# Where the operands of TensorE's products begin in SBUF: alike modulo 512 bytes, or 64 bytes apart

## The chip, the core and the metric

The kernel runs on one core of a Trainium2 chip. The metric is the device time of one execution in microseconds; a comparison takes the median of several runs. TensorE (PE) multiplies a stationary operand of up to 128 columns, which a weight load (PEld) brings into the array, with a moving operand of up to 512 columns that is streamed past it. The sums go to PSUM. VectorE (DVE), ScalarE (ACT) and GpSimd (POOL) do the elementwise work, and SyncE (SP) issues most transfers.

## The reference

A decoder trunk of two layers over 512 tokens of width 1024, in float32. Both layers have an adaptive RMSNorm, a mixer, a residual, a second adaptive RMSNorm, a SwiGLU feed-forward of hidden width 2816 and a residual:

```python
h = rmsnorm(x, norm_mix_g[layer]) * (1.0 + scale_m) + shift_m
mixed = attention_head_groups(h, ...) if layer % 2 == 0 else gated_deltanet(h, ...)
x = x + gate_m * mixed
h = rmsnorm(x, norm_ffn_g[layer]) * (1.0 + scale_f) + shift_f
gate, up = jnp.split(h @ ffn_w_in[layer], 2, axis=-1)
x = x + gate_f * ((silu(gate) * up) @ ffn_w_out[layer])
```

Layer 0 mixes with 8 block-sparse and 8 stick-breaking attention heads, layer 1 with a gated delta rule of 8 heads (projections q, k, v, z, a short convolution, a triangular inverse for each block, a scan over four chunks of 128 tokens).

## The kernel before

Everything is held transposed, features on partitions and 512 tokens along the free dimension. A float32 product is made of three products of rounded float32 values (type fp32r): every operand is split into a high and a low part, and the kernel adds high×high (line 330), high weight×low activation (line 331) and low weight×high activation (line 333). A weight chunk is 1024 features × 128 outputs, eight slices `wh[:, k]` and `wl[:, k]` of 512 bytes to a partition, so it takes 24 products of 512 columns each, or 48 of 256 columns where a product is done in two halves of the tokens (`HALVES`).

`weight_plan` lists all chunks in order. `fetch` loads each into a `raw` tile (SP's queue), ACT writes `wh` (line 247) and DVE or POOL writes `wl` (lines 249 to 252). Tiles `raw` (3 buffers), `wh` and `wl` (2 each) are in the pool `wpool`. Chunks that are needed in both halves are kept in the pool `keep` on the right side of SBUF. For layer 0's attention the chunks are fetched by POOL (`eng == "d"`), and every third pair takes two `raw` buffers in place of `wh` and `wl`.

The activations: `hs` (tiles `hh`, `hl`, right side of SBUF) is the normalised input of layer 0's mixer, of layer 0's feed-forward and of the delta-net; in layer 1's feed-forward its tiles hold the first 8 hidden chunks. `hs1` (`h1h`, `h1l`, left side) is the input of layer 1's feed-forward, and `ah`, `al` (left side) are the hidden chunks of both feed-forwards. The attention's outputs and values are `ah`, `al`, `bh`, `bl`, also on the left.

A tile's address is the sum of what stands before it in its pool stack. In the built program of the kernel before:

- on the left (the weights in `wpool`, `h1h`, `ah` and the like) tiles begin at 32 modulo 512 bytes;
- on the right `hs` begins at 480 modulo 512, and so do the kept weights.

Offsets inside the tiles (a weight slice, a half of the tokens, a block of 128 tokens) are multiples of 512 bytes. So in `hs` times weights the stationary operand begins 64 bytes further on than the moving one (modulo 512), in `h1h` or `ah` times weights both begin alike, and where a weight is the moving operand and `hs` the stationary one (`vproj`, `zproj`, lines 711 to 713 and 1109 to 1111) the stationary one begins 64 bytes earlier.

The 512-column products with `hs` against weights are 12 chunks of the attention's projections, 40 of layer 0's feed-forward input, 22 of the delta-net's projections, and 8 of the 22 hidden chunks in 7 of 8 output chunks of layer 1's feed-forward.

Of the kernel before, what the change touches and what calls it, by code (L numbers as in the profile page):

```python
# [8 lines left out]
F32 = mybir.dt.float32  # L9
# [4 lines left out]
OP = mybir.AluOpType  # L14
# [43 lines left out]


AHEAD = 2  # L60
LAG = 3
# [16 lines left out]
def weight_plan(I):  # L78

    p = []

    def add(key, src, kc=KC, n=128, eng="a", keep=False):
        p.append((key, src, kc, n, eng, keep))

    def out(name, src, nsplit, parts, keep, spare=()):
        order = list(range(KC - nsplit)) + (1 if keep or spare else 2) * list(range(KC - nsplit, KC))
        for n in order:  # L90
            for a, b in parts:
                add((name, n, a), src[n][:, a:b], b - a,
                    keep="h" if n in spare else keep and n >= KC - nsplit)

# [6 lines left out]
    def vproj(name, i, eng="a"):  # L101
        for j in (0, 4):
            add((name, i, j), I[name][i][:, j:j + 4], 4, 256, eng)

# [9 lines left out]
    for i in 2 * first:  # L114
        add(("gdn_in", i), I["gdn_in"][i], eng=EK0)
    for i in range(8 + NFIRST_GDN, 16):
# [9 lines left out]
    for i in range(2):  # L126
        for n in range(KC):
            add(("gdn_out", n, 0), I["gdn_out"][n])
    ffn(1)
# [3 lines left out]
def build(nc, tc, I, O):  # L133
# [3 lines left out]
    with ctx:  # L137
# [50 lines left out]
        G.memset(ones, 1.0)  # L188
        epsc = const.tile([128, 2], F32, name="epsc")
        G.memset(epsc[:, 0:1], EPS)  # L190
        G.memset(epsc[:, 1:2], math.pi / 2)
        eps = epsc[:, 0:1]
        ident = cst("ident")
# [30 lines left out]
        G.tensor_tensor(adabg, adab1[:, 8:16], gmix[:, 0:8], op=OP.mult)  # L224

# [44 lines left out]
        def w_pair(keep, kc, n, turn=False):  # L270

            if turn:
                turns[0] += 1
            tags = (("raw", 3),) * 2 if turn and turns[0] % 3 == 0 else (("wh", 2), ("wl", 2))
            return [kpool[0].tile([128, kc, n], F32R, name=t, tag=t, bufs=4) if keep else
                    wpool.tile([128, kc, n], F32R, name=t, tag=tag, bufs=bufs)
                    for t, (tag, bufs) in zip(("wh", "wl"), tags)]

        def fetch():
            _, dram, kc, n, eng, keep = plan[len(loaded)]  # L280
            if eng == "d":

                h, l = w_pair(keep, kc, n, True)
                dmas.append(nc.gpsimd.dma_start(h, dram).ins)
# [6 lines left out]
            if keep == "h":  # L291
# [9 lines left out]
                return  # L301
            h, l = w_pair(keep, kc, n)
            split(raw, h, l, eng)
# [225 lines left out]
def attention(e, x0ctx):  # L529
    nc, tc, V, G, A, PE, I = e.nc, e.tc, e.V, e.G, e.A, e.PE, e.I  # L530
    from contextlib import ExitStack
    with ExitStack() as ctx:
# [203 lines left out]
        def moba(pair, h, q, k):  # L736

            ph = work.tile([128, 1920], F32R, name="ph", tag="ph", bufs=1)
            pl = work.tile([128, 1920], F32R, name="pl", tag="pl", bufs=1)
            for i in range(4):  # L740
# [22 lines left out]
                e.split(src, *(x[:, i * 128:i * 128 + 384 * (i + 1)].rearrange("p (j q) -> p j q", q=384)[:, :, :128]  # L763
                               for x in (ph, pl)))
            pv_out(pair, h * 64, "m", ph, pl, lambda x, j: x[:, 512 * j:512 * j + 512 - 128 * j])
# [537 lines left out]
```

## Time and profile before

| | |
|---|---|
| median of 3 runs | 1423.26 us (1421.87 to 1425.09) |
| the profiled execution | 1422.44 us |
| its span in the trace | 1420.7 us |
| mean granted TensorE clock | 0.986 of full speed |
| PE busy | 1374.8 us, 97% of the span, 7354 products |
| DVE, ACT, POOL busy | 819.5, 605.7, 291.5 us |

A product's busy time in the trace overlaps that of the next one, so a product's pace is read from start to start: the distance between the starts of two products, divided by the number of products from the one to the other. Windows of the span are given in microseconds from its start.

### The profile page before, as it was taken

What the parts mean: (1) busy time and instruction counts of PE and PEld (TensorE: products, weight loads), DVE (VectorE), ACT (ScalarE), POOL (GpSimd) and SP (SyncE); (2) the same over time, 40 slices, a digit from 0 to 9 for tenths busy, and PEclk for the clock granted to TensorE, in tenths of its full rate; (3) what the DMA queues carried; (4) which work ended last, traced back from release to release, by engine and by line L of the source; (5) the groups of instructions that cost most, each with busy time, mean ns of one, the idle gap of its engine ahead of it and who ended that gap; (6) DMA issues with size and microseconds to landing.
All of it is one profiled execution on the core that took longest, in us unless ns stands there. A gap on an engine that the chain in (4) does not pass through costs nothing.

```text
span 1420.7 us, 19227 instructions
## 1 busy us (share of the span) xinstructions
PE 1374.8 (97%) x7354; PEld 1161.3 (82%) x7354; DVE 819.5 (58%) x1422; ACT 605.7 (43%) x1162; POOL 291.5 (21%) x280
## 2 busy tenths in 40 slices
PE   7899999899999999999999999999999999999997
PEld 4797777798888888889888778888998888888887
DVE  6777879654666666423777796446783333333233
ACT  5577888743222222223556643346662222222222
POOL 4024443110111111000024834311001111110010
PEclk8999999999999999999999999999999999999999
DMA  9437664141666676434522324312451323333332
GB/s 370 157 79 191 178 176 150 53 154 60 208 213 235 224 242 219 129 108 140 163 85 75 90 69 124 100 50 90 143 185 60 104 89 104 91 102 93 95 99 70
DMA packets 58734, 190.66 MB, mean 134 GB/s; under 512 B 7081, under 2 KB 11305, under 8 KB 58642
## 3 DMA queue, kind: packets, MB, share of 16 engines
q1 hardware_dynamic: 53376, 173.56, 37.7%
q0 software_dynamic: 4112, 14.82, 4.7%
q8 instruction: 58, 0.95, 0.3%
q10 hardware_dynamic: 1154, 1.05, 0.2%
q14 instruction: 34, 0.28, 0.1%
HBM read 184.11 MB, written 5.29 MB: 133 GB/s over the span
## 4 chain that ended last, share of the span: by engine, by line
PE 84%; DVE 5%; ACT 4%; DMA 3%; POOL 1%; issue 1%; SPq 0%; DVEq 0%; ACTq 0%; POOLq 0%
PE mm L330 21%; PE mm L331 21%; PE mm L333 21%; DMA wh<-in_attn_in_dram 2%; PE f L331 1%; PE f L330 1%; PE f L333 1%; PE mm L1111 1%; PE mm L1109 1%; PE mm L1110 1%; PE bank L943 1%; DVE DT L1003 1%; DMA call<-in_consts_dram 1%; PE bank L1045 1%; PE mm L712 1%
## 5 line engine op out<-in xcount | busy, mean ns | idle before, releaser
L247 ACT ACTIVATE wh<-raw 128x1024 fp32r<-128x1024 f32 (+1 forms) x203 | 211.4, 1041 | 544.1 <-PE mm L331 503.6
L252 DVE TENSOR_TENSOR wl<-raw,wh 128x1024 fp32r<-128x1024 f32 (+1 forms) x193 | 231.9, 1202 | 195.6 <-ACT wh L247 178.4
L330 PE MATMUL mm<-hh,wh 128*128 128x512 f32 (+1 forms) x776 | 292.6, 381 | 1.2 <-ACT wh L247 0.6
L331 PE MATMUL mm<-hl,wh 128*128 128x512 f32 (+1 forms) x776 | 291.0, 378 | 0.0
L333 PE MATMUL mm<-hh,wl 128*128 128x512 f32 (+1 forms) x776 | 245.7, 377 | 0.0
L330 PEld LDWEIGHTS mm<-hh,wh 128*128 128x128 f32 x776 | 146.7, 189 | 28.4 <-ACT wh L247 1.1
L331 PEld LDWEIGHTS mm<-hl,wh 128*128 128x128 f32 x776 | 146.5, 189 | 27.5
L333 PEld LDWEIGHTS mm<-hh,wl 128*128 128x128 f32 x776 | 141.9, 188 | 28.6
L249 POOL TENSOR_SCALAR ah<-ac 128x512 fp32r<-128x512 f32 x36 | 53.2, 1478 | 372.8 <-DVE ac L490 372.8
L212 DVE CUSTOM_DVE_ANT_0 aw<-aw,cond 128x1024 f32<-128x1024 f32 x96 | 126.2, 1332 | 5.8 <-DMA aw<-in_ada_w_dram 5.7
L331 PE MATMUL mm<-al,wh 128*128 128x512 f32 (+1 forms) x354 | 124.6, 356 | 0.0
L330 PE MATMUL mm<-h1h,wh 128*128 128x512 f32 x320 | 124.5, 389 | 0.0
L331 PE MATMUL mm<-h1l,wh 128*128 128x512 f32 x320 | 124.5, 389 | 0.0
L330 PE MATMUL mm<-ah,wh 128*128 128x512 f32 (+1 forms) x354 | 124.2, 356 | 0.2 <-ACT ah L247 0.2
L490 DVE TENSOR_TENSOR ac<-sg,mm 128x512 f32<-128x512 f32 x40 | 27.5, 688 | 152.4 <-PE mm L333 152.4
L333 PE MATMUL mm<-h1h,wl 128*128 128x512 f32 x320 | 105.0, 389 | 0.0
L333 PE MATMUL mm<-ah,wl 128*128 128x512 f32 (+1 forms) x354 | 104.1, 356 | 0.0
L330 PEld LDWEIGHTS mm<-ah,wh 128*128 128x128 f32 x354 | 66.7, 189 | 10.0 <-ACT ah L247 0.5
L331 PEld LDWEIGHTS mm<-al,wh 128*128 128x128 f32 x354 | 66.8, 189 | 9.5
L333 PEld LDWEIGHTS mm<-ah,wl 128*128 128x128 f32 x354 | 64.2, 189 | 9.5
L330 PEld LDWEIGHTS mm<-h1h,wh 128*128 128x128 f32 x320 | 60.1, 188 | 12.6
L333 PEld LDWEIGHTS mm<-h1h,wl 128*128 128x128 f32 x320 | 60.0, 188 | 12.5
(396 smaller groups left out, 2492.0 us busy)
## 6 DMA issues: line engine op xcount, KB each, us to landing
aw<-in_ada_w_dram SPq DMA_DIRECT2D x96, 512.0 KB
raw<-in_ffn_in_dram SPq DMA_DIRECT2D x88, 512.0 KB
raw<-in_ffn_out_dram SPq DMA_DIRECT2D x36, 512.0 KB
raw<-in_gdn_in_dram SPq DMA_DIRECT2D x26, 512.0 KB
raw<-in_gdn_z_dram SPq DMA_DIRECT2D x16, 512.0 KB
raw<-in_gdn_out_dram SPq DMA_DIRECT2D x16, 512.0 KB
raw<-in_ffn_out_dram SPq DMA_DIRECT2D x18, 384.0 KB
wh<-in_attn_in_dram POOLq DMA_DIRECT2D x12, 512.0 KB, 4.7
```

The costliest lines, as they stand in the source:

```text
L212: return V.tensor_tensor_reduce(w, w, cond, 1.0, 0.0, OP.mult, OP.add, mod[:, j:j + 1])
L247: ins = A.activation(h, src, AF.Copy)
L249: G.tensor_scalar(h, src, 1.0, 1.0, op0=OP.mult, op1=OP.mult)
L252: (G if eng == "p" else V).tensor_tensor(l, src, h.bitcast(F32), op=OP.subtract)
L330: PE.matmul(ps, wh[k][:, 0], xh[:, cs], start=first and i == 0, stop=False)
L331: PE.matmul(ps, wh[k][:, 0], xl[:, cs], start=False, stop=False)
L333: PE.matmul(ps, wl[j][:, 0], x[j][0][:, cs], start=False, stop=last and j == order[-1])
L490: ins = V.tensor_tensor(ac, sg, pu, op=OP.mult)
L712: PE.matmul(ps, xh[:, t], wl, start=False, stop=False)
L943: PE.matmul(ps[:, c], lhs[:, cs], rhs[:, cs], start=True, stop=True)
L1003: V.tensor_tensor(d, DS[:, :m, m:m + 1].to_broadcast([128, m, w]), DV[:, m:m + 1, m:].to_broadcast([128, m, w]), op=OP.mult)
L1045: PE.matmul(p4[:, c], U[h][lo, c], x[lo, c, lo], start=True, stop=True)
```

## The change

It adds 288 bytes of padding (`gap`) to the constants, takes a column of `epsc` and 88 columns of `adab1` away that nothing reads, and adds 448 bytes ahead of `keep`. With that every tile on the left moves from 32 to 480 modulo 512, and the kept weights from 480 to 32. The buffers `wh` and `wl` in `wpool` grow from 4096 to 4608 bytes, and a chunk begins `at` bytes into its buffer: 0 for the products of 512 columns, 64 for those of 256 columns, and 448 in `vproj`, where the weight is the moving operand. The output projections give `at=64` from chunk `KC - nsplit` on (the halves). To make room, `moba`'s tiles `ph` and `pl` shrink from 1920 to 1664 columns; their blocks stay where they were. No engine's order of instructions changes; POOL has one memset less.

After it, in the built program: `hs`, `h1h`, `ah` and all 512-column weights begin at 480 modulo 512; weights that are stationary in 256-column products begin at 32 (480 + 64); in `vproj` the moving weight begins at 416 and `hs` at 480. One case goes the other way: in the last output chunk of layer 1's feed-forward (`keep="h"`, 256 columns) the weights lie in `hs1`'s tiles. Before, they stood 64 bytes past `hs` for 8 of its hidden chunks (48 products), after it alike.

```diff
+GAP, GAP_KEPT = 288, 448
...
-    def add(key, src, kc=KC, n=128, eng="a", keep=False):
-        p.append((key, src, kc, n, eng, keep))
+    def add(key, src, kc=KC, n=128, eng="a", keep=False, at=0):
+        p.append((key, src, kc, n, eng, keep, at))
...
-                    keep="h" if n in spare else keep and n >= KC - nsplit)
+                    keep="h" if n in spare else keep and n >= KC - nsplit, at=64 if n >= KC - nsplit else 0)
...
-            add((name, i, j), I[name][i][:, j:j + 4], 4, 256, eng)
+            add((name, i, j), I[name][i][:, j:j + 4], 4, 256, eng, at=448)
...
     for i in 2 * first:
-        add(("gdn_in", i), I["gdn_in"][i], eng=EK0)
+        add(("gdn_in", i), I["gdn_in"][i], eng=EK0, at=64)
...
-            add(("gdn_out", n, 0), I["gdn_out"][n])
+            add(("gdn_out", n, 0), I["gdn_out"][n], at=64)
...
-        epsc = const.tile([128, 2], F32, name="epsc")
-        G.memset(epsc[:, 0:1], EPS)
-        G.memset(epsc[:, 1:2], math.pi / 2)
-        eps = epsc[:, 0:1]
+        eps = const.tile([128, 1], F32, name="eps")
+        G.memset(eps, EPS)
+
+        const.tile([128, GAP // 4], F32, name="gap")
...
-        adab1 = const.tile([128, 96], F32, name="adab1")
-        G.tensor_scalar(adab1, adab, 1.0, 1.0, op0=OP.mult, op1=OP.add)
+        adab1 = const.tile([128, 8], F32, name="adab1")
+        G.tensor_scalar(adab1, adab[:, 8:16], 1.0, 1.0, op0=OP.mult, op1=OP.add)
...
+            gap = kctx[0].enter_context(tc.tile_pool(name="gap", bufs=1, side="right"))
+            gap.tile([128, GAP_KEPT // 4], F32, name="gap")
             kpool[0] = kctx[0].enter_context(tc.tile_pool(name="keep", bufs=1, side="right", reuse_waits="tile"))
...
+            if keep:
+                return [kpool[0].tile([128, kc, n], F32R, name=t, tag=t, bufs=4) for t in ("wh", "wl")]
+            if turn and turns[0] % 3 == 0:
+                return [wpool.tile([128, kc, n], F32R, name=t, tag="raw", bufs=3) for t in ("wh", "wl")]
+            room = [wpool.tile([128, KC * 128 + 128], F32R, name=t, tag=t, bufs=2) for t in ("wh", "wl")]
+            return [t[:, at // 4:at // 4 + kc * n].rearrange("p (a b) -> p a b", b=n) for t in room]
```

## Rows read from the trace of the kernel before

**Rows 1.** The page: the span, TensorE's share, the chain that ended last.
```profile
span 1420.7 us, 19227 instructions
PE 1374.8 (97%) x7354; PEld 1161.3 (82%) x7354; DVE 819.5 (58%) x1422; ACT 605.7 (43%) x1162; POOL 291.5 (21%) x280
...
PE 84%; DVE 5%; ACT 4%; DMA 3%; POOL 1%; issue 1%; SPq 0%; DVEq 0%; ACTq 0%; POOLq 0%
```

**Rows 2.** Stages by windows: window, length, busy us by engine (count), granted clock, DMA.
```profile
core 0: us, PE busy (x) PEld busy (x) DVE busy (x) ACT busy (x) POOL busy (x), PEclk, DMA share, GB/s
...
40.00:67.00 27.00, 27.00 (x118) 21.84 (x117) 21.11 (x31) 13.26 (x24) 0.83 (x1) 1.00 0.48 153
...
100.00:293.00 193.00, 180.36 (x970) 146.25 (x970) 144.59 (x286) 147.73 (x333) 71.92 (x80) 1.00 0.56 157
...
345.00:567.00 222.00, 222.00 (x955) 178.93 (x954) 140.97 (x193) 51.01 (x59) 29.67 (x20) 1.00 0.64 215
...
811.00:876.00 65.00, 59.02 (x278) 48.27 (x277) 57.73 (x103) 26.64 (x41) 27.91 (x16) 0.95 0.30 91
...
1072.00:1290.00 218.00, 218.00 (x963) 180.48 (x962) 74.06 (x81) 52.10 (x60) 29.71 (x21) 1.00 0.30 94
```

**Rows 3.** The chain, 512-column products: start us, us, what.
```profile
354.27 0.93 PE mm L333 x4
...
567.07 0.93 PE mm L333 x4
...
597.04 0.91 PE mm L333 x4
...
656.88 0.91 PE mm L333 x4
...
1076.00 0.91 PE mm L333 x4
...
1184.80 0.91 PE mm L333 x4
1293.73 0.93 PE mm L333 x4
...
1369.43 0.93 PE mm L333 x4
```

**Rows 4.** Timeline of PE, `zproj`: start us, us, engine, line, what.
```profile
871.51 0.40 PE L1109 MATMUL mm<-wh,hh 128*128 128x512 f32 x1
...
874.04 0.39 PE L1111 MATMUL mm<-wl,hh 128*128 128x512 f32 x1
```

**Rows 5.** Timeline of PE, products of 256 columns in four places.
```profile
313.53 0.28 PE L330 MATMUL mm<-ah-1_176,wh 128*128 128x256 f32 x1
...
315.89 0.28 PE L333 MATMUL mm<-ah,wl 128*128 128x256 f32 x1
...
318.74 0.28 PE L330 MATMUL f<-hh,wh 128*128 128x256 f32 x1
...
319.70 0.28 PE L333 MATMUL f<-hh,wl 128*128 128x256 f32 x1
...
673.88 0.28 PE L330 MATMUL mm<-ah,wh 128*128 128x256 f32 x1
...
675.92 0.28 PE L333 MATMUL mm<-ah,wl 128*128 128x256 f32 x1
...
1014.57 0.62 PE L333 MATMUL mm<-hh,wl 128*128 128x256 f32 x4
...
1017.29 0.62 PE L333 MATMUL mm<-hh,wl 128*128 128x256 f32 x4
```

**Rows 6.** Windows of line 330 alone: PE busy us (count).
```profile
712.00:779.00 67.00, 31.27 (x78) 1.00 0.25 79
779.00:811.00 32.00, 13.55 (x33) 1.00 0.29 82
811.00:876.00 65.00, 26.62 (x65) 0.95 0.30 91
```

**Rows 7.** The chain of 100 to 293 us, shares by line.
```profile
by line: DMA wh<-in_attn_in_dram 11.5%; PE mm L330 7.0%; PE mm L331 6.8%; PE mm L333 6.5%; issue 6.3%; PE z L792 3.1%; ACT wl L285 2.8%; DVE aw L212 2.6%; PE o L723 2.5%; PE o L725 2.5%; ACT p L748 2.4%; ACT ph L247 2.3%; PE o L724 2.3%; DV
```

**Rows 8.** Timeline of the triangular inverse and its ends: POOL, DVE, transfer, PE.
```profile
781.11 3.10 POOL L983 TENSOR_SCALAR vp<-uv 32x128 f32<-32x128 f32 x8 [0.64 <-DVE uv L980]
...
811.25 0.16 POOL L999 MEMSET vp<- 128x32 f32 x1
...
811.45 0.21 DVE L1003 TENSOR_TENSOR DT<-vp 128x31 f32<-128x31 f32 x1 [2.91 <-POOL vp L999]
...
860.04 0.19 DVE L1005 TENSOR_TENSOR vp<-vp,DT 128x31 f32<-128x31 f32 x1
...
871.68 0.69 DVE L1018 TENSOR_TENSOR uv<-vp,call 128x512 f32<-128x512 f32 x1 [0.69 <-DMA vp<-dr]
...
875.86 0.38 PE L1028 MATMUL bank<-xinv,um 128*128 128x128 f32 x1 [1.43 <-DVE xinv L1022]
```

**Rows 9.** Timeline of PE, the second half of layer 0's first feed-forward chunks.
```profile
330.72 1.01 PE L330 MATMUL f<-hh,wh 128*128 128x256 f32 x4 [1.84 <-ACT hh L397]
```

More of the change, by code (lines that the diff above doesn't have):

```diff
@@ L218, in modcol @@
             return fin[:, j:j + 1]
-        adab1 = const.tile([128, 96], F32, name="adab1")
-        G.tensor_scalar(adab1, adab, 1.0, 1.0, op0=OP.mult, op1=OP.add)
+        adab1 = const.tile([128, 8], F32, name="adab1")
+        G.tensor_scalar(adab1, adab[:, 8:16], 1.0, 1.0, op0=OP.mult, op1=OP.add)
         adabg = const.tile([128, 8], F32, name="adabg")
-        G.tensor_tensor(adabg, adab1[:, 8:16], gmix[:, 0:8], op=OP.mult)
+        G.tensor_tensor(adabg, adab1, gmix[:, 0:8], op=OP.mult)
         def ada_fin1(comp, k):
@@ L264, in open_keep, with w_pair @@
             kctx[0] = ExitStack()
+            gap = kctx[0].enter_context(tc.tile_pool(name="gap", bufs=1, side="right"))
+            gap.tile([128, GAP_KEPT // 4], F32, name="gap")
             kpool[0] = kctx[0].enter_context(tc.tile_pool(name="keep", bufs=1, side="right", reuse_waits="tile"))
         turns = [0]
-        def w_pair(keep, kc, n, turn=False):
+        def w_pair(keep, kc, n, at, turn=False):
             if turn:
                 turns[0] += 1
[L274 to L277, printed above, removed]
+            if keep:
[4 more added lines that the diff above has]
+            return [t[:, at // 4:at // 4 + kc * n].rearrange("p (a b) -> p a b", b=n) for t in room]
         def fetch():
-            _, dram, kc, n, eng, keep = plan[len(loaded)]
+            _, dram, kc, n, eng, keep, at = plan[len(loaded)]
             if eng == "d":
-                h, l = w_pair(keep, kc, n, True)
+                h, l = w_pair(keep, kc, n, at, True)
                 dmas.append(nc.gpsimd.dma_start(h, dram).ins)
@@ L301, in fetch @@
                 return
-            h, l = w_pair(keep, kc, n)
+            h, l = w_pair(keep, kc, n, at)
             split(raw, h, l, eng)
@@ L736, in moba @@
         def moba(pair, h, q, k):
-            ph = work.tile([128, 1920], F32R, name="ph", tag="ph", bufs=1)
-            pl = work.tile([128, 1920], F32R, name="pl", tag="pl", bufs=1)
+            ph = work.tile([128, 1664], F32R, name="ph", tag="ph", bufs=1)
+            pl = work.tile([128, 1664], F32R, name="pl", tag="pl", bufs=1)
             for i in range(4):
@@ L762, in moba @@
                 src = pt[:, :n].rearrange("p (j q) -> p j q", q=128)
-                e.split(src, *(x[:, i * 128:i * 128 + 384 * (i + 1)].rearrange("p (j q) -> p j q", q=384)[:, :, :128]
-                               for x in (ph, pl)))
+                e.split(src, *(x.rearrange("p (j q) -> p j q", q=128)[:, i:4 * i + 1:3] for x in (ph, pl)))
             pv_out(pair, h * 64, "m", ph, pl, lambda x, j: x[:, 512 * j:512 * j + 512 - 128 * j])
```

## The prediction

> **What bounds the kernel now.** I read the page first: TensorE is busy 97% of the span, and 84% of the chain that ended last is on it [rows 1]. Shares are averages, so the windows came next [rows 2]. [...] From 100 to 293 us (attention) PE is busy 180.36 of 193.00 us and ACT and DVE about 145 each: a mixed chain. From 811 to 876 us DVE is busy 57.73 of 65.00 us and PE waits.
>
> So the question is what sets the pace. The chain gives it from start to start [rows 3]. In layer 0's feed-forward input (`hs` against weights, stationary operand 64 bytes further on) equal rows stand at 354.27 and 567.07 us with 38 chunks of 24 products between: 212.80 / 912 = 233.3 ns. In layer 1's (`h1h`, begins like the weights) they stand at 1076.00 and 1184.80 us, 20 chunks: 108.80 / 480 = 226.7 ns. The engines, shapes and clock are the same. The two output projections show it side by side: 66 products take 14.96 us in layer 0 (656.88 − 597.04, four chunks) where all operands begin alike, and 15.14 us in layer 1 (1369.43 − 1293.73, five chunks) where 24 of the 66 have `hs` as moving operand; the 0.18 us are 7.5 ns for each of the 24. At 256 columns it is the other way round [rows 5]: alike, 17 starts from 673.88 to 675.92 us are 120.0 ns apart; with the stationary operand 64 bytes on, 24 starts from 1014.57 to 1017.29 us are 113.3 ns apart. With the stationary operand 64 bytes earlier it is 230.0 ns at 512 columns (11 starts from 871.51 to 874.04 us [rows 4]) and 118.0 at 256 (20 starts from 313.53 to 315.89 us [rows 5]).
>
> I take it that the two start addresses modulo 512, one against the other, set the pace, and not the place of either: `hs` at 480 against kept weights at 480 paces 256 columns at 120.0 ns (8 starts from 318.74 to 319.70 us [rows 5]), the same as `ah` at 32 against weights at 32, and `hs` against weights at 32 paces them at 113.3.
>
> [...]
>
> **The change part by part.** A product gains 6.7 ns (233.3 to 226.7) at 512 columns with `hs`.
>
> - Layer 0's feed-forward input: 40 chunks × 24 = 960 products, PE saturated: 6.4 us.
> - Layer 1's feed-forward output: 7 chunks × 0.18 = 1.2 us.
> - Delta-net projections: 528 products. From 712 to 779 us line 330 alone runs 78 times [rows 6], so all three lines about 231 times, less 24 for the narrow a/b weights, whose offsets only turn round: 207 × 6.7 = 1.4 us, up to where POOL's copies start at 781.11 us [rows 8]. From there on a chain runs that holds no projection: POOL to 811.25, the 31 steps of DVE from 811.45 to 860.04, two transfers to 871.68, then DVE and the first product of the levels at 875.86 us, before which PE already waits 1.43 us. About (33 + 65) × 3 = 294 products lie beside it [rows 6]: 2.0 us that I count at nothing, for PE would just wait 3.4 us in place of 1.43. That is its upper bound. What is late next there is the DVE loop, as before.
> - Attention projections: 288 products, 1.9 us if all count, nothing if none. Lines 330, 331 and 333 hold 20.3% of the chain in 193 us, 39 us [rows 7], of which the attention's output chunks, alike already, take about 15; 24 us / 0.2333 is about 100 products, 0.7 us. I take 0.8.
> - Start: 118 products from 40 to 67 us with PE full [rows 2], about half with `hs` moving (6.7 ns), half with the weight moving (230.0 to 226.7, 3.3 ns): 0.6 us. Before 40 us PE waits for other work; nothing.
> - `zproj`: 192 products × 3.3 ns, less the 12 before the wait at 875.86: 0.6 us.
>
> At 256 columns the pace with 64 bytes is not one number: 113.3 ns is one chunk. I bound the gain from alike by 6.7 ns and, by the 118.0 of the other sign, by 2.0, and take 4.6, near the middle, because no row tells which chunk is typical (115.4 ns then).
>
> - Layer 0's feed-forward output, 264 products from 120.0 to 115.4: 1.2 us (0.5 to 1.8).
> - Attention output 192, layer 1's first feed-forward chunks 192, `vproj` 192, all from 118.0 to 115.4: 0.5 + 0.5 + 0.4 (0 to 2.7).
> - Layer 0's first feed-forward chunks, 192 products from 120.0: 0.9 us, but the first half lies before PE's wait of 1.84 us for the norm [rows 9], so 0.45.
> - The 48 products that lose their 64 bytes: −0.2 us.
>
> The rest costs nothing. POOL's memset less and the shorter add fall into the start, where transfers and the norm bind. The 4608-byte buffers hold the same bytes and the same writes; their only price is space. If ACT or DVE wrote slower at other addresses, which no row shows, it would be hidden: ACT is busy 51 of 222 and DVE 141 of 222 us in the longest stage [rows 2]; should that cover go, PE would wait there.
>
> Sum: 6.4 + 1.2 + 1.4 + 0.8 + 0.6 + 0.6 + 1.2 + 1.4 + 0.45 − 0.2 = 13.85 us. The profiled execution took 1422.44 us, so 1408.6; the median of the runs lies 0.82 higher, and I forecast **1409.4 us**, 1.0% faster. Differences within 0.2% (2.8 us) can't be told from none.
>
> **The rivals.**
>
> *All of it pays.* The 2.0 us beside the inverse, 1.1 more in attention, 0.4 in the start, 0.45 in the first chunks and the upper bounds at 256 columns (0.6 + 1.3) make 19.7 us: 1403.6 us. Against it stand the chains off PE in [rows 7, 8].
>
> *Only the saturated stages pay.* 6.4 + 1.2 + 1.4 + 0.5 − 0.2 = 9.3 us: 1414.0. For it: PE's slack in the other stages is filled by waits for ACT and DVE, which a faster PE only lengthens. Longer waits may also lower the clock: from 811 to 876 us, around a wait, the granted clock averages 0.95 against 1.00 [rows 2].
>
> *The moving operand's own place sets the pace* (the other side). At 480 (`hs`) 512 columns pace 233.3, at 32 (`h1h`, `ah`) 226.7. The change takes `h1h`, `ah` and the attention's outputs to 480: (320 + 242 + 20) × 3 = 1746 products would lose 6.7 ns, 11.7 us, `zproj` 0.6 more, all in saturated stages, and `hs` would gain nothing: 1423.3 + 12.3 = 1435.6 us. It decides from 1.6 ns a product on, where 1746 of them eat the 2.85 us that the 256-column terms give (1.2 + 1.4 + 0.45 − 0.2). Against it: the one tile `hs` at 480 has both paces at 256 columns, 120.0 and 113.3 [rows 5].
>
> *The addresses do not set the 512-column pace*, but something else that `hs` has, such as lying far up in SBUF. The 256-column terms alone might stay, 2.85 us, or nothing: 1420.4 to 1423.3, in the middle 1421.8. For it: no row has `hs` alike at 512 columns. [...] Against it, again the 256 columns, where `hs` alike behaves as `ah` alike.
>
> **How the numbers follow.** My forecast has 0.67; all of it pays 0.10; only the saturated stages 0.10; no effect at 512 columns 0.08; slower by the moving operand's place 0.05. The first three are faster: 0.87; the fourth is the same: 0.08; slower 0.05. The range takes in the forecast with its bounds and most of the next two cases, 1404 to 1415 us, and leaves the last two out.
>
> **What would show it.** In the changed kernel's chain, equal L333 rows in layer 0's feed-forward input should stand 5.44 us apart, as in layer 1's, in place of 5.60, and that stage should be 6.4 us shorter; layer 1's input should be as long as before. The output chunks of layer 1 should take 14.96 us. Chunks of `gdn_out` at 256 columns should stay as they are, and layer 0's output halves fall from 120.0 to between 113 and 118 ns. PE's wait before the first L1028 should grow by about 2 us, with the DVE loop as long as before. I am wrong if layer 1's feed-forward slows down, if layer 0's keeps 5.60 us, or if waits in attention eat more than the 1.9 us that it could gain.

## The result and the profile after

| | before | after |
|---|---|---|
| median | 1422.94 us (6 runs) | 1411.55 us (6 runs, 1410.65 to 1413.18) |
| ratio, 95% interval | | 0.992 [0.9907, 0.9933] |
| profiled execution | 1422.44 us | 1410.65 us |

The change saves 11.4 us by the medians and 11.8 between the two profiled executions, where the prediction summed 13.85 us. The time lies in the range that was given. Line numbers of the changed kernel stand 6 or 7 above those of before in the places spoken of here (L330, L331, L333 are now L337, L338, L340).

The page of the changed kernel, beside [rows 1]: the counts are those of before but for three instructions, the shares of the chain are within one per cent of those of before, and TensorE's busy time is 13.9 us less.

```profile
span 1408.8 us, 19224 instructions
PE 1360.9 (97%) x7354; PEld 1158.4 (82%) x7354; DVE 818.6 (58%) x1422; ACT 605.4 (43%) x1162; POOL 292.0 (21%) x279
...
PE 84%; DVE 6%; ACT 4%; DMA 3%; POOL 1%; issue 1%; SPq 0%; DVEq 0%; ACTq 0%; POOLq 0%
```

Its chain at four rows that answer to [rows 3] (start us, us, what): layer 0's feed-forward input 38 chunks apart, layer 1's feed-forward output 5 chunks apart.

```profile
352.82 0.91 PE mm L340 x4
...
559.54 0.91 PE mm L340 x4
...
1282.80 0.91 PE mm L340 x4
...
1357.60 0.91 PE mm L340 x4
```

The 38 chunks of layer 0 take 206.72 us where they took 212.80: 5.44 a chunk in place of 5.60, 226.7 ns a product in place of 233.3, and 40 × 0.16 = 6.4 us for the stage. The five output chunks of layer 1 take 74.80 us in place of 75.70; a chunk is 14.96, as in layer 0.

Four windows between the same products as in the kernel before (columns as in [rows 2]): the start, layer 0's first feed-forward chunks, its input, and the stage of the inverse.

```profile
40.70:68.42 27.72, 27.72 (x118) 22.77 (x117) 20.90 (x30) 12.62 (x23) 0.83 (x1) 0.95 0.45 145
...
316.72:343.78 27.06, 25.22 (x206) 24.65 (x204) 15.75 (x32) 12.82 (x23) 0.62 (x1) 1.00 0.25 79
343.78:559.60 215.82, 215.82 (x955) 178.73 (x954) 141.05 (x193) 51.09 (x60) 29.77 (x20) 1.00 0.66 221
...
800.25:867.09 66.84, 59.53 (x276) 49.56 (x275) 56.58 (x103) 26.65 (x41) 29.28 (x16) 0.92 0.31 91
```

Three of them show something beside the pace. The start did not get shorter (27.72 us; 27.00 for as many products in [rows 2]), but its granted clock averages 0.95 where it was 1.00. The first chunks of layer 0 took 1.94 us less, much more than their products could give. And from 800 to 867 us, where nothing was to be gained, 2 us were lost: 66.84 against some 65 in [rows 2]. Of these, 1.4 us lie ahead of DVE's first step of the inverse, because PE now reaches the window's first product earlier against it: 1.65 us ahead of that step (800.25 and 801.90 us), where it was 0.25 us ahead of it (811.20 and 811.45).

The window of the first chunks in the kernel before, at a granted clock of 0.94:

```profile
316.00:345.00 29.00, 27.16 (x205) 26.46 (x204) 15.77 (x32) 12.81 (x23) 0.62 (x1) 0.94 0.24 74
```

The timeline of PE at the products of 256 columns in layer 0's output halves (stationary operand 64 bytes on):

```profile
650.04 0.28 PE L337 MATMUL mm<-ah,wh 128*128 128x256 f32 x1
...
664.29 0.28 PE L338 MATMUL mm<-al,wh 128*128 128x256 f32 x1
664.41 0.59 PE L364 MATMUL mm<-ssq,ones 128*128 128x256 f32 x2
...
675.19 0.28 PE L340 MATMUL mm<-ah,wl 128*128 128x256 f32 x1
...
680.63 0.28 PE L340 MATMUL mm<-ah,wl 128*128 128x256 f32 x1
```

121 starts up to 664.29 us are 117.8 ns apart. Then two products of the norm come between, and 48 starts from 675.19 to 680.63 are 113.3 apart. Tiles, distance and clock are the same: one address distance has two paces here.

Last, the inverse in the changed kernel (timeline of PE, POOL and DVE), with the first full q/k/v product as a mark; it answers to [rows 8].

```profile
702.66 0.40 PE L338 MATMUL mm<-hl,wh 128*128 128x512 f32 x1
...
789.25 1.80 POOL L998 DMA_DIRECT2D dr<-vp  x1 [0.31 <-POOL vp L989]
...
796.60 0.60 POOL L999 DMA_DIRECT2D vp<-dr  x1 [1.84 <-DMA dr<-vp]
...
801.90 0.21 DVE L1009 TENSOR_TENSOR DT<-vp 128x31 f32<-128x31 f32 x1 [4.23 <-POOL vp L1005]
...
851.19 0.19 DVE L1011 TENSOR_TENSOR vp<-vp,DT 128x31 f32<-128x31 f32 x1
...
863.80 1.80 DVE L1024 TENSOR_TENSOR uv<-vp,call 128x512 f32<-128x512 f32 x1 [1.66 <-DMA vp<-dr]
...
866.88 0.38 PE L1034 MATMUL bank<-xinv,um 128*128 128x128 f32 x1 [1.82 <-DVE xinv L1028]
```

And three rows of the kernel before at the same places, which [rows 8] lacks:

```profile
712.08 0.40 PE L331 MATMUL mm<-hl,wh 128*128 128x512 f32 x1
...
799.73 1.80 POOL L992 DMA_DIRECT2D dr<-vp  x1 [0.31 <-POOL vp L983]
...
806.15 0.61 POOL L993 DMA_DIRECT2D vp<-dr  x1 [0.91 <-DMA dr<-vp]
```

From the mark to DVE's first step it is 99.24 us after and 99.37 before (811.45 − 712.08), so almost nothing came of a stage full of faster products. POOL waits 1.84 us for the first transfer in place of 0.91. From the end of DVE's last step (851.38 us; 860.23 before) to the returned blocks it is 12.42 us in place of 11.45. The transfers themselves have become slower (the first landed 7.1 us after its issue in place of 6.1, the last 7.4 in place of 6.4). The later return does not reach PE in this pair, though: its first product of the levels starts 15.50 us after DVE's last step (866.88 − 851.38), before it was 15.63 (875.86 − 860.23). The loop of DVE between took 49.48 us in place of 48.78; it takes 48.4 to 49.6 us in the executions of all kernels here.

### The profile page after: what moved, and what is told of

Its sections match the earlier page's. It is cut to its first block, busy times and chain, and to the rows that moved or that the text cites. A ratio compares the mean times of both kernels' runs of the same rounds, so it can differ in the third digit from the quotient of the medians.

```text
span 1408.8 us, 19224 instructions
## 1 busy us (share of the span) xinstructions
PE 1360.9 (97%) x7354; PEld 1158.4 (82%) x7354; DVE 818.6 (58%) x1422; ACT 605.4 (43%) x1162; POOL 292.0 (21%) x279
## 3 DMA queue, kind: packets, MB, share of 16 engines
q10 hardware_dynamic: 1154, 1.05, 0.2%
## 4 chain that ended last, share of the span: by engine, by line
PE 84%; DVE 6%; ACT 4%; DMA 3%; POOL 1%; issue 1%; SPq 0%; DVEq 0%; ACTq 0%; POOLq 0%
PE mm L337 21%; PE mm L338 21%; PE mm L340 21%; DMA wh<-in_attn_in_dram 1%; PE f L340 1%; PE f L338 1%; PE f L337 1%; PE mm L1117 1%; PE mm L1115 1%; PE mm L1116 1%; PE bank L949 1%; DVE DT L1009 1%; DMA call<-in_consts_dram 1%; PE bank L1051 1%; PE mm L719 1%
## 5 line engine op out<-in xcount | busy, mean ns | idle before, releaser
L254 DVE TENSOR_TENSOR wl<-raw,wh 128x1024 fp32r<-128x1024 f32 (+1 forms) x193 | 231.9, 1202 | 192.1 <-ACT wh L249 176.0
L337 PE MATMUL mm<-hh,wh 128*128 128x512 f32 (+1 forms) x776 | 290.0, 377 | 0.7 <-ACT wh L249 0.6
L338 PE MATMUL mm<-hl,wh 128*128 128x512 f32 (+1 forms) x776 | 288.0, 374 | 0.0
L340 PE MATMUL mm<-hh,wl 128*128 128x512 f32 (+1 forms) x776 | 243.2, 374 | 0.0
L337 PEld LDWEIGHTS mm<-hh,wh 128*128 128x128 f32 x776 | 146.6, 189 | 25.2 <-ACT wh L249 1.1
L338 PEld LDWEIGHTS mm<-hl,wh 128*128 128x128 f32 x776 | 146.9, 189 | 24.2
L340 PEld LDWEIGHTS mm<-hh,wl 128*128 128x128 f32 x776 | 142.7, 189 | 25.2
L338 PE MATMUL mm<-h1l,wh 128*128 128x512 f32 x320 | 124.5, 389 | 0.0
L337 PE MATMUL mm<-h1h,wh 128*128 128x512 f32 x320 | 124.5, 389 | 0.0
L338 PE MATMUL mm<-al,wh 128*128 128x512 f32 (+1 forms) x354 | 124.0, 355 | 0.0
L337 PE MATMUL mm<-ah,wh 128*128 128x512 f32 (+1 forms) x354 | 123.7, 355 | 0.2 <-ACT ah L249 0.2
L340 PE MATMUL mm<-h1h,wl 128*128 128x512 f32 x320 | 105.0, 389 | 0.0
L340 PE MATMUL mm<-ah,wl 128*128 128x512 f32 (+1 forms) x354 | 103.8, 355 | 0.0
L337 PEld LDWEIGHTS mm<-ah,wh 128*128 128x128 f32 x354 | 66.5, 188 | 9.9 <-ACT ah L249 0.5
L338 PEld LDWEIGHTS mm<-al,wh 128*128 128x128 f32 x354 | 66.6, 188 | 9.4
L340 PEld LDWEIGHTS mm<-ah,wl 128*128 128x128 f32 x354 | 63.9, 188 | 9.4
L338 PEld LDWEIGHTS mm<-h1l,wh 128*128 128x128 f32 x320 | 60.1, 188 | 12.5
L337 PEld LDWEIGHTS mm<-h1h,wh 128*128 128x128 f32 x320 | 60.0, 188 | 12.5
```

What stands on the lines that cost most here:

```text
L254: (G if eng == "p" else V).tensor_tensor(l, src, h.bitcast(F32), op=OP.subtract)
L337: PE.matmul(ps, wh[k][:, 0], xh[:, cs], start=first and i == 0, stop=False)
L338: PE.matmul(ps, wh[k][:, 0], xl[:, cs], start=False, stop=False)
L340: PE.matmul(ps, wl[j][:, 0], x[j][0][:, cs], start=False, stop=last and j == order[-1])
```

## Experiments

Each edit is one to the changed kernel, unless it says otherwise. Distances are those of the stationary operand's start past the moving one's.

**e1, the changed kernel again**, no edit.

> The changed kernel once more, for a second profile. The first profile gained 6.3 us in layer 0's feed-forward input and 1.2 us in layer 1's output, as forecast, but lost 1.4 us up to 67 us and 2.0 us between the start of DVE's inverse loop and the first product of the levels, where it was forecast to gain 0.6 and lose nothing. Theory L (where the half-clock stretches fall is chance): in a second profile the half-clock stretches lie elsewhere, the stages of pure products (layer 0's input 215.8 us, layer 1's output 93.8 us) repeat within 0.2 us, and the start or the inverse stage differs by 1 us or more from the first profile. Theory S (the faster products bring these losses with them): both stages repeat within 0.3 us and half-clock stretches lie at the same places.

One execution of 1410.89 us. The time of the stages of pure products came back to the hundredth of a microsecond (215.82 us in layer 0's input), as both theories had it. The stretch at half clock in the start came back at 41.0 us (40.3 in the first profile, granted 0.50 up to 43.7); products from 41.35 us on start 0.43 us apart, where those just before start 0.23 to 0.24 apart. The stage of the inverse took 0.4 us more than in the first profile. Of the 2.0 us that the expectation puts between DVE's first step and the first product of the levels, only 0.57 lay there in the first profile (64.98 us against 64.41); the rest lay ahead of that step.

**e2, the products of 512 columns alone**: the others get their old distances back, apart from the attention's output halves, which are alike here (and `open_keep` takes 0 in layer 0, 64 in layer 1).

```diff
-    keep="h" if n in spare else keep and n >= KC - nsplit, at=64 if n >= KC - nsplit else 0)
+    keep="h" if n in spare else keep and n >= KC - nsplit, at=0)
...
-            add((name, i, j), I[name][i][:, j:j + 4], 4, 256, eng, at=448)
+            add((name, i, j), I[name][i][:, j:j + 4], 4, 256, eng, at=64)
```

> The change for 512-column products alone: all of them alike modulo 512 as in the changed kernel; the 256-column products keep their distances of before (delta-net output and its first projections 64, vproj and layer 1's first feed-forward chunks the stationary operand 64 earlier, layer 0's output halves and first chunks alike), but for the attention's output halves, which are alike (before: 64 earlier; 192 products at 118.0 to 120.0 ns, 0.4 us worse). Theory A (both widths pay, each by its pace): 2.3 us of the 11.4 us belong to the 256-column products, so 1411.6 + 2.3 + 0.4 = 1414.3 us, ratio to before 0.994. Theory W (only the wide products pay, the 256-column stages gained by the clock): 1411.6 to 1412.0 us, ratio 0.992.

**e3, the products of 256 columns alone**: `hs` against 512-column weights is 64 bytes apart again, and the attention's output halves are alike (`open_keep` takes 384 in layer 1).

```diff
-GAP, GAP_KEPT = 288, 448
+GAP, GAP_KEPT = 352, 448
...
-            add((name, i, j), I[name][i][:, j:j + 4], 4, 256, eng, at=448)
+            add((name, i, j), I[name][i][:, j:j + 4], 4, 256, eng, at=384)
...
-            add(("gdn_out", n, 0), I["gdn_out"][n], at=64)
+            add(("gdn_out", n, 0), I["gdn_out"][n], at=0)
...
-        sm = gp.tile([128, 17, C4, HG], F32, name="sm")
+        sm = gp.tile([128, 16, C4, HG], F32, name="sm")
```

> The change for 256-column products alone: their distances as in the changed kernel (64), but for the attention's output halves, which are alike; 512-column products keep the distances of before (hs 64, weights moving in zproj 64 earlier, the others alike). A small tile that nothing reads is left out to make room. Theory A: 1422.9 - 2.3 + 0.4 = 1421.0 us, ratio 0.9987, and layer 0's feed-forward input at 5.60 us a chunk as before. Theory W: 1422.9 us, ratio 1.000. If the gains of e2 and e3 add up to that of the whole change (11.4 us, less the 0.4 us that each lacks twice), the two parts are independent.

e2 took 1415.12 us (0.9949 [0.9937, 0.9962]), e3 1417.83 (0.9971 [0.9961, 0.9981]): by the kernel before in the same series, 1422.88, they save 7.8 and 5.0 us, together 12.8 where the whole saves 11.4. Windows of layer 0's feed-forward input and of the second part of its output halves, in e2 and then in e3 (between the same products, 222.14 and 18.96 us before, 215.82 and 18.08 after):

```profile
345.52:561.35 215.83, 215.83 (x955) 178.80 (x954) 140.98 (x193) 51.10 (x60) 29.71 (x20) 1.00 0.66 221
665.22:684.18 18.96, 18.96 (x157) 18.85 (x156) 14.71 (x25) 13.08 (x21) 0.11 (x1) 1.00 0.62 182
```

```profile
343.49:565.61 222.12, 222.12 (x956) 179.01 (x954) 141.01 (x193) 51.11 (x60) 29.76 (x20) 1.00 0.64 215
669.28:687.50 18.22, 18.22 (x157) 18.11 (x156) 14.28 (x24) 13.16 (x20) 0.11 (x1) 1.00 0.60 181
```

In these windows each half moves its own stage and leaves the other's where it was before. The address distance is the cause, in both widths. e2's time is near its first theory's (1414.3 us). e3 saved more than either theory gave it (1421.0 or 1422.9), and two things in it and in e2 are not the products' pace. One is the granted clock in layer 0's first chunks: e2 has the old distance there (alike), and takes, between the same products as the 29.00 us of before,

```profile
318.02:345.52 27.50, 25.66 (x205) 25.08 (x204) 15.59 (x32) 12.81 (x23) 0.62 (x1) 1.00 0.27 78
```

So 1.50 us of the 1.94 are the clock, and 0.44 (27.50 − 27.06) the products. The gain by the clock is in e2, in e3 and in the whole change, so it counts twice in the 12.8. The other is the place of the delta-net's tiles (see e10 and e12): in e3 they begin at 384 modulo 512 and not at 448.

**e4, a sweep of distances**, in steps of 64 bytes over layer 0 and of 16 over layer 1.

```diff
-        for j in first + [j + f for f in range(NFIRST, FC) for j in (0, FC)]:
-            add(("ffn_in", l, j), I["ffn_in"][l, j], keep=j in first)
+        for c, j in enumerate(first + [j + f for f in range(NFIRST, FC) for j in (0, FC)]):
+            add(("ffn_in", l, j), I["ffn_in"][l, j], keep=j in first, at=16 * ((c - 4) % 32) if l else 64 * ((c - 4) % 8))
...
-            add(("gdn_out", n, 0), I["gdn_out"][n], at=64)
+            add(("gdn_out", n, 0), I["gdn_out"][n], at=64 * n)
```

> The changed kernel with other offsets of the weights, chunk by chunk: layer 0's feed-forward input (512 columns, hs moving) steps the distance of stationary from moving operand by 64 bytes from 0 to 448, five times round; layer 1's (512 columns, h1 moving) by 16 bytes from 0 to 496; the delta-net's output (256 columns, hs moving) by 64 bytes, twice round; zproj (512 columns, weight moving) by 64 bytes. Theory R (the distance modulo 512 sets the pace): the chunk time in layer 0 repeats every eight chunks; distance 0 gives 5.44 us for 24 products (226.7 ns), 64 gives 5.60 (233.3), 448 gives 5.52 (230.0), and the other five lie between 5.4 and 5.7, each the same in all five rounds within 0.03 us; layer 1 has the same time at the same distance. Theory P (the moving operand's or the weight's own place, or its place in SBUF, sets it): with hs and h1 left where they are all chunks of a layer take the same time (5.44), or layer 0 and layer 1 differ at the same distance. The sweep also says whether any distance beats 5.44 us at 512 columns or the 113 ns at 256.

One execution, 1419.97 us. The chain of layer 1's input; the last group of each chunk stands 24 products from that of the next. The chunks that end at the second to fifth row have distances of 240, 256, 272 and 288 bytes:

```profile
1147.80 0.93 PE mm L340 x4
1153.28 0.91 PE mm L340 x4
1158.72 0.91 PE mm L340 x4
1164.16 0.92 PE mm L340 x4
1169.74 0.93 PE mm L340 x4
```

5.48, 5.44, 5.44, 5.58 us a chunk. All distances in nanoseconds a product, from the starts within a chunk (256 to 496 bytes repeat the row within 0.6):

```
bytes  0     16    32    48    64    80    96    112   128   144   160   176   192   208   224   240
ns     227.3 226.7 233.1 233.3 233.1 231.8 233.9 233.3 233.5 233.4 233.2 229.8 228.9 233.3 233.4 227.5
```

So 512 columns were fast (226.7 to 227.5 ns) within 16 bytes of alike, modulo 256 and not 512, and cost 2 to 7 ns more elsewhere (228.9 to 233.9). At 256 columns the steps of 64 gave 119.2 alike, 116.8 at 64, 118.2 at 128 and 117.1 at 192 (means within four chunks each; at 64 bytes one of them settled at 113.3 and one at 117.8).

**e5, the delta-net's q, k and v products apart again** (528 products at 64 bytes); **e6, the kernel before once more**; **e7, 256 columns in steps of 16 bytes**.

```diff
-        add(("gdn_in", i), I["gdn_in"][i], eng=EK)
+        add(("gdn_in", i), I["gdn_in"][i], eng=EK, at=64)
```

(e5; the lines with `EQ` and `EV` alike.)

```diff
-            add(("gdn_out", n, 0), I["gdn_out"][n], at=64)
+            add(("gdn_out", n, 0), I["gdn_out"][n], at=16 * (8 * i + n))
```

(e7; the 12 pieces of layer 0's output halves at `16 * (2 + piece)`.)

> The changed kernel, but the 22 weight chunks of the delta-net's q, k and v projections begin 64 bytes further on than hs again (528 products of 512 columns, at 233.3 ns in place of 226.7). My theory now: what these products gain is taken back, because from the first copy of POOL on, before the triangular inverse, the work up to the inverse's end is a chain of POOL, DVE and transfers that the products only stand beside. Then the stage of 712 to 779 us takes 1.1 us longer again and that of 811 to 876 us 1 to 2 us less, and the whole takes 1411.5 to 1412.2 us, at most 0.5 us over the changed kernel. The prediction counted 1.4 us for these products: 1412.9. A rival, that all 528 products pay in full and what was lost near 811 us was a chance placing of a stretch at half clock: 3.5 us, 1415.0.

> The kernel before once more, for a second profile. It tells whether three things of the first profile belong to that kernel or to one execution of it: 40 to 67 us took 26.94 us there and 27.7 to 28.1 in every changed kernel; 811 to 876 us took 64.88 us and 65.5 to 67.3 in the others; and a stretch at half clock stood at 331 us, which no changed kernel had. If they belong to the kernel (theory one: the change moved when PE waits, and so where the clock falls), all three come back within 0.3 us. If the half-clock stretches fall by chance (theory two), at least one of them moves and the stage that loses or gains one changes by 1 to 2 us, with the whole within 1421.9 to 1425.1 us.

> The changed kernel, but the 16 chunks of the delta-net's output (48 products of 256 columns each, hs moving) begin 0, 16, 32 up to 240 bytes further on than hs, modulo 256, and the 12 pieces of layer 0's feed-forward output halves (24 or 18 products of 256 columns, ah moving) 32, 48 up to 208 bytes. In the sweep by 64 bytes 256 columns paced at 119.4 ns alike, 115.2 with 64, 118.6 with 128 and 118.0 with 192. Theory one: what counts is one narrow place, as at 512 columns (within 16 bytes of alike), so that one or two steps near 64 lie at 113.3 or below and all others at 117 to 120. Theory two: the pace falls and rises smoothly between 0 and 128, with its least at 64 and 115 to 117 at 32 and 96. Either way the whole is 1 to 2 us above the changed kernel: 1412.5 to 1413.5.

e5 took 1413.89 us (1409.54 to 1416.12; 0.9942 [0.9929, 0.9956]), too scattered to decide; it was run again as e10. But its profile has a start without a fall of the clock, and e6 (1424.57 us) one with:

```profile
39.84:66.15 26.31, 26.31 (x118) 21.77 (x116) 21.01 (x31) 13.10 (x24) 0.83 (x1) 1.00 0.48 154
```

```profile
41.46:70.34 28.88, 28.88 (x117) 23.21 (x116) 20.38 (x30) 12.66 (x23) 0.88 (x1) 0.93 0.42 134
...
319.80:348.80 29.00, 27.16 (x205) 26.38 (x204) 15.75 (x32) 12.80 (x23) 0.62 (x1) 0.94 0.23 74
```

The start of the kernel before takes 27.00 or 28.88 us, and with these addresses 26.31 or 27.72, by whether the clock falls there: at full clock the 118 products gain about 0.65 us, as forecast, and a fall of the clock, in some executions of both kernels, added 1.4 us (granted 0.95, after) and 1.9 us (0.93, e6). Layer 0's first chunks at 29.00 us with a clock of 0.94 came back in the kernel before; in the changed kernel, e2 and e11 the clock was 1.00 there, and of the twelve executions of the changed kernel and its variants only e12 had a fall. Why the clock falls there was not settled, nor whether the change keeps it from falling.

e7 took 1413.43 us. Neither theory of it holds: all distances gave 116.6 to 120 ns, in an irregular order of single steps, except 64 and 192. There a run of products settled to 117.8 or to 113.3 and kept it until something interrupted: 64 ran at 113.4 in one piece and at 117.8 in others, 192 at 118.0 in one stage and 113.3 in another.

**e8, steps of 4 bytes around 64 and 192.**

```diff
-            add(("gdn_out", n, 0), I["gdn_out"][n], at=64)
+            add(("gdn_out", n, 0), I["gdn_out"][n], at=(52, 180)[i] + 4 * n)
```

(The 12 pieces of layer 0's output halves at 68, 60, 72, 56, 76, 52, 188, 196, 184, 200, 192, 64.)

> The changed kernel, with the 16 chunks of the delta-net's output at 52, 56 up to 80 and 180, 184 up to 208 bytes past hs, and the 12 pieces of layer 0's feed-forward output halves at 68, 60, 72, 56, 76, 52, 188, 196, 184, 200, 192 and 64 bytes. The sweep in steps of 16 showed that 64 and 192 alone have two settled paces, 113.3 and 117.8 ns, and that a run of products keeps the one that it falls into. Theory one: the two paces belong to exactly these places (a multiple of 64), and any step of 4 off them gives the unsettled 117 to 119 ns of 48 and 80. Theory two: only the 32 bytes in which a start lies count, so that 64 to 76 (and 192 to 204) behave as 64 does and 52 to 60 as 48. Theory three: some place within 12 bytes has the fast pace alone, 113.3 in every piece; then the products of 256 columns at 117.8 in the changed kernel (the attention's output, the first pieces of both feed-forwards, about half of the delta-net's output) could gain 4.5 ns each. The whole at 1411 to 1413.5 us by all three.

One execution, 1410.14 us. Theory three held, at 76 bytes. Starts within a piece, in nanoseconds from one to the next, at three distances:

```
72 (653.58 us) 122 116 115 120 117 120 117 115 118 122 120 118 122 116
76 (658.53 us) 124 122 118 119 118 113 114 113 113 114 113 113 114 113
64 (677.63 us) 117 118 117 118 118 117 119 117 118 118 118 117 118 118
```

At 76 (and, after more products, at 52) a piece fell into 113.3; at 64 it stayed where it fell first (117.8 in the row above); at 56, 60, 68 and 72 it settled on neither.

**e9, the changed kernel timed again, beside e10, e5 timed again, and e11, all 256-column weights at 76 bytes.** e9 and e10 have no new edit.

```diff
-                return [kpool[0].tile([128, kc, n], F32R, name=t, tag=t, bufs=4) for t in ("wh", "wl")]
+                kept = [kpool[0].tile([128, KC * 128 + 128], F32R, name=t, tag=t, bufs=4) for t in ("wh", "wl")]
+                return [t[:, 3:3 + kc * n].rearrange("p (a b) -> p a b", b=n) for t in kept]
...
-            add(("gdn_out", n, 0), I["gdn_out"][n], at=64)
+            add(("gdn_out", n, 0), I["gdn_out"][n], at=76)
```

(`vproj` at 436, all other 64 at 76.)

> The changed kernel unaltered, timed beside the next two and against the kernel before in the same rounds. By the earlier runs 1411.5 us and a ratio of 0.992.

> The delta-net's 528 products at 64 bytes once more, now timed beside the changed kernel. Its first median, 1413.89 us, stood 2.3 us over the changed kernel's of another series, while the profiled execution of it took 1409.54, less than the changed kernel's 1410.65. In the profiles so far 712 to 876 us took 163.3 to 164.8 us in five executions with these products alike and 164.0 to 165.0 in four with them apart, means of 164.05 and 164.57. Theory (the chain of POOL, DVE and transfers takes the gain): 0.5 us over the changed kernel, at most 1. As the prediction counted: 1.4 us over it. Rival (all 528 products pay): 3.5 us over it.

> The changed kernel with every weight of 256-column products 76 bytes from hs and the like in place of 64 (the kept weights in larger tiles, vproj at the same distance); the last output chunk of layer 1 stays alike. The sweep by 4 bytes had two pieces at 76 and both ran at 113.3 ns, one from its first product and one after the sixth. Theory: at 76 a run of products always falls to 113.3 within about ten products, wherever it comes from. Then the attention's output (192 products at 117.8) gains 0.8 us, layer 0's first feed-forward pieces 0.4 to 0.8, layer 0's feed-forward halves 0.5 (their first 122 at 117.8), the delta-net's output up to 0.6 and vproj 0.2: 2.5 us less than the changed kernel, 1409.0. Rival: the two pieces at 76 had the right neighbours by chance, 76 is unsettled like 72 and 80 at 118.5; then pieces now at 113.3 lose 5 ns, some 400 products: 2 us more, 1413.5, with the first feed-forward pieces of layer 1 (113.8 now) at 118.

e9: 1412.72 us, 0.9930 [0.9917, 0.9943]. e10: 1412.93, 0.9936 [0.9924, 0.9948]. e11: 1411.04, 0.9923 [0.9910, 0.9937]. The three can't be told apart by their times; their stages can. e11's windows of the attention's output halves and of layer 0's first chunks:

```profile
294.43:316.64 22.21, 22.21 (x195) 22.11 (x194) 13.48 (x26) 10.33 (x18) 3.46 (x2) 1.00 0.35 114
316.64:342.95 26.31, 24.47 (x206) 23.90 (x204) 16.07 (x32) 12.81 (x23) 0.62 (x1) 1.00 0.27 83
```

The changed kernel has 23.01 and 27.06 us there, so e11 takes 0.80 and 0.75 less, and 0.48 less in layer 0's first output halves. Nearly every piece at 76 ran at 113.3 within some ten products; one run of about 45 products in `gdn_out` stayed at 120.0 after an interruption. The whole stage of `gdn_out` gained nothing (42.09 us between the same products, 41.98 in the changed kernel).

The delta-net in e10, from the mark to DVE's first step:

```profile
703.49 0.39 PE L338 MATMUL mm<-hl,wh 128*128 128x512 f32 x1
...
803.75 0.21 DVE L1009 TENSOR_TENSOR DT<-vp 128x31 f32<-128x31 f32 x1 [3.77 <-POOL vp L1005]
```

100.26 us, 1.02 more than the changed kernel's 99.24. So my theory of e5 and e10, that a chain of POOL, DVE and transfers takes the products' gain whatever they do, fell: the products pay 1 us up to there, and something else costs as much in the changed kernel as against the kernel before (99.37 with slow products). The landing of the transfers names it. The inverse's four transfers, one by one in order of time (KB each, us from issue to landing), before and after:

```profile
dr<-vp POOLq DMA_DIRECT2D x1, 512.0 KB, 6.1
vp<-dr POOLq DMA_DIRECT2D x1, 512.0 KB, 4.5
dr<-vp POOLq DMA_DIRECT2D x1, 512.0 KB, 2.9
vp<-dr POOLq DMA_DIRECT2D x1, 512.0 KB, 6.4
```

```profile
dr<-vp POOLq DMA_DIRECT2D x1, 512.0 KB, 7.1
vp<-dr POOLq DMA_DIRECT2D x1, 512.0 KB, 4.5
dr<-vp POOLq DMA_DIRECT2D x1, 512.0 KB, 2.9
vp<-dr POOLq DMA_DIRECT2D x1, 512.0 KB, 7.4
```

The first and the fourth land about 1 us later, the second and the third do not.

The delta-net's `vp` tiles follow the padded constants too: in the built programs they begin at 0 modulo 512 before, at 448 after (small tiles ahead of them in their pool put them off the 32 and 480 of the others). All four move blocks of 32 × 32 float32. By the kernel's access patterns the first and the fourth do it in pieces of 128 bytes, and the second and the third take 4096 bytes of a partition in one piece.

**e12, e11 with the delta-net's tiles 64 bytes earlier**, `vp` at 384.

```diff
-        sm = gp.tile([128, 17, C4, HG], F32, name="sm")
-        gg, lnb, beta, gc, gl, cb, lu, kdc, nbr, egl, kk, qq, epq, t0, t1, oss, ors = (sm[:, i] for i in range(17))
+        sm = gp.tile([128, 16, C4, HG], F32, name="sm")
+        gp.tile([128, 16], F32, name="pad")
+        gg, lnb, beta, gc, gl, cb, lu, kdc, nbr, egl, kk, qq, epq, t0, oss, ors = (sm[:, i] for i in range(16))
```

> The kernel with 76 bytes, and the delta-net's tiles (vp, uv, the inverse's buffers) begin 64 bytes earlier (an unused 128 bytes of sm dropped, 64 of padding put in): vp at 384 modulo 512, a multiple of 128, in place of 448. The kernel before had vp at 0. The page of every profile so far gives the inverse's transfers a median of 4.5 or 4.6 us to landing (dr<-vp) and 5.4 or 5.5 (vp<-dr) in the three executions with vp at a multiple of 128 (the kernel before twice, the narrow half alone) and 5.0 and 5.8 to 6.0 in the ten with vp at 448, whatever the products' pace. Theory: the transfers in pieces of 128 bytes pay for the 64 bytes off. Then they land in 4.5 and 5.4 again, POOL's wait for the first falls from 1.8 to 0.9 us, from the end of DVE's 31 steps to its first work on the returned blocks takes 11.3 us in place of 12.2 to 12.5, the time from POOL's first copy to the first product of the levels falls by 1.8 us to some 132, and the whole to 1409.2 us. Rival: the transfers are slower because a faster PE shifts what else the queues carry; they stay at 5.0 and 5.9, and the whole at 1411.0.

1409.23 us (4 runs, 1408.68 to 1409.89), 0.9902 [0.9886, 0.9919], the lowest median of all. e11, the same without the move, saved 11.0 us in its own series (1422.05 − 1411.04) where e12 saves 14.3 (1423.56 − 1409.23), but the two intervals overlap, so the stage decides. The first and the fourth transfer, and the timeline:

```profile
dr<-vp POOLq DMA_DIRECT2D x1, 512.0 KB, 6.2
...
vp<-dr POOLq DMA_DIRECT2D x1, 512.0 KB, 6.2
```

```profile
703.65 0.39 PE L339 MATMUL mm<-hl,wh 128*128 128x512 f32 x1
...
796.69 0.60 POOL L1001 DMA_DIRECT2D vp<-dr  x1 [0.98 <-DMA dr<-vp]
...
801.97 0.21 DVE L1011 TENSOR_TENSOR DT<-vp 128x31 f32<-128x31 f32 x1 [3.29 <-POOL vp L1007]
...
851.25 0.19 DVE L1013 TENSOR_TENSOR vp<-vp,DT 128x31 f32<-128x31 f32 x1
...
862.64 0.69 DVE L1026 TENSOR_TENSOR uv<-vp,call 128x512 f32<-128x512 f32 x1 [0.44 <-DMA vp<-dr]
...
866.20 0.49 PE L1036 MATMUL bank<-xinv,um 128*128 128x128 f32 x3
```

The transfers are as short as before, POOL's wait is 0.98 us, the way back 11.20 (862.64 − 851.44). With products alike or apart and `vp` at a multiple of 128 or not, from the mark to DVE's first step:

| us | `vp` at 0 or 384 | `vp` at 448 |
|---|---|---|
| products 64 apart | 99.37 (before), 99.45 (e3) | 100.30 (e5), 100.26 (e10) |
| products alike | 98.32 (e12) | 99.24 (after), 99.23 (e11) |

Both effects are there and add up: the products give 1.05 us, the tiles' place takes 0.9. They also lie apart in time: up to the issue of the first transfer it is 86.5 to 86.6 us in all nine executions with the products alike and 87.6 to 87.7 in the five with them apart, and from there to DVE's first step 11.7 to 11.8 us in the four with `vp` at 0 or 384 and 12.6 to 12.65 in the ten at 448.

On the way back the tiles' place takes another 1.1 us up to DVE's first work on the blocks (11.2 to 11.45 us at 0 or 384 in four executions, 12.1 to 12.55 at 448 in ten; means 11.30 and 12.38). Only about half of it reaches PE. From DVE's last step to the first product of the levels it is, with the products apart, 15.4 to 15.6 us in three executions at 0 or 384 and 16.0 in two at 448; with them alike, 14.76 in e12 and 15.5 to 16.6 in eight at 448. From the mark to that product e12 takes 162.55 us (866.20 − 703.65); the eight take 163.1 to 165.1.

## Why the prediction was right, and where its sum was off

The mechanism held: it is the two starts against each other that set the pace, and neither's own place (e2, e3, e4): alike, 512 columns pace at 226.7 ns with both at 32 (before) and with both at 480 (after). So the two rivals without a gain at 512 columns fall: `hs` alike paces at 226.7 ns, and layer 1's input kept its pace at 480. Of the rivals within the gain, all of it pays (1403.6 us) and only the saturated stages pay (1414.0), neither came: several stages around waits paid too, but the delta-net's inverse took back what its products gave. That it is modulo 512 was too wide: at 512 columns the pace repeated every 256 bytes, within 0.6 ns (e4).

**Layer 0's feed-forward input**, 6.4 us: right (6.4). **Layer 1's output**, 1.2: right (0.18 for each of the chunks, 74.80 against 75.70 for five). **Layer 0's output halves**, 1.2: right in sum (1.16 between the same products), by two paces and not by a middle one. **Layer 1's first chunks**, 0.5: right (0.5). **The loss** in the last chunk, 0.2: right (0.16).

**Attention's output**, 0.5: nothing. Its distance was turned round, its pace stayed 117.8. The step that failed is "I bound the gain from alike by 6.7 ns and, by the 118.0 of the other sign, by 2.0, and take 4.6": there is no typical pace of 115.4, but two, and which one a run falls into was not to be had from the rows. The kernel before already had both at 64 bytes: in `gdn_out` 48 starts from 1005.01 to 1010.66 us are 117.7 ns apart, close before the 113.3 of [rows 5].

**Start**, 0.6: right at full clock (27.00 to 26.31), hidden in the profile by a fall of the clock (0.95; 0.93 in e6) that came and went in both kernels.

**Layer 0's first chunks**, 0.45: 1.94, of which 0.44 are the products, as counted, and 1.50 the granted clock (0.94 before, 1.00 in e2), which no term had. **Attention's projections**, 0.8, **`vproj`**, 0.4, and **`zproj`**, 0.6, can't be read: the executions scatter more than that there (192.1 to 194.4 us for the attention).

**Delta-net projections**, 1.4 up to POOL's copies: 1.05 up to DVE's first step, so about right, and what was counted at nothing (the products beside the loop) was rightly counted so: from DVE's first step to the first product of the levels the eight executions with the products alike and `vp` at 448 take 64.8 us in the mean, the two with them apart (e5, e10) 65.0. PE's wait ahead of the levels was to grow by 2 us and grew from 1.43 to 1.82; PE's other waits in the stage took the rest (7.3 us idle of 66.84, against 6.0 of 65.00 in [rows 2]).

The step that failed is "The rest costs nothing. ... their only price is space." The padding moves every tile behind it, and two of the inverse's transfers to and from `vp` pay for it: 0.9 us before the loop, all of it on the way to DVE's first step, and 1.1 behind it, of which about half reaches PE. In the two profiled executions the way from the mark to the first product of the levels was to become 1.4 us shorter and became 0.44 longer (164.22 us against 163.78): the products gave 1.05, POOL's longer wait took 0.93 (1.84 − 0.91), the loop took 0.70, which is within its scatter, and 0.13 came back behind it.

That the whole came within 2.5 us of the sum is in part luck with the clock. Up to 67 us 1.4 us were lost where 0.6 were to be gained, and the first chunks gave 1.5 us that no term had. e12, which takes the transfers' loss back and has 76 bytes besides, saves 14.3 us in its series.

What makes the pieces of 128 bytes land later with `vp` at 448 than at 0 or 384 no run here shows. The runs show the landing times alone: out of the tile 7.1 us against 6.1 (before) and 6.2 (e12), and no change where 4096 bytes go in one piece.

## What to carry to other kernels

Read the pace of products from start to start, by group of operands and not over the kernel; where equal shapes at equal clock differ, compare the starts of both operands modulo 256 bytes (here 226.7 ns alike against 233.3 at 64 bytes, at 512 columns). A padding that shifts one pool shifts every tile behind it: list the transfers that use these tiles, and look at their landing times, before the gain is summed. And where an expected gain is missing in a stage, a small table of the two suspects, each with and without, tells more than the time of the whole kernel.

## What the runs showed of the hardware

At 256 columns runs of float32 (fp32r) products had two settled paces at one distance, 113.3 and 117.8 ns at 64 bytes (after; 117.7 and 113.3 before), and in these rows kept the one that they fell into until other products came between. At 76 bytes nearly every run came to 113.3 (e11). Alike they were 120.0 ns apart (before). 113.3 is half of the 226.7 of 512 columns alike, so per column both reached the same pace, 0.443 ns, at different distances.

A transfer of 512 KB in pieces of 128 bytes landed about 1 us later when its tile in SBUF began 64 bytes past a multiple of 128: 7.0 to 7.1 us after its issue in ten executions with `vp` at 448 against 6.1 to 6.2 in four at 0 or 384 (out of the tile), 7.1 to 7.5 against 6.2 to 6.5 (into it). Transfers of the same tiles in pieces of 4096 bytes landed as before (4.2 to 4.5 and 2.9 us in all).
